# Strassen's seven block products for both matmuls of a gated MLP

## The chip, the core and the metric

The kernel runs on one core of a Trainium2 chip. The core has five engines with queues of their own: TensorE (matmuls from SBUF into PSUM), VectorE, ScalarE, GpSimd (elementwise work; GpSimd has no path to PSUM) and SyncE, whose queue issues all DMA transfers here. The metric is device time in microseconds, the median of three runs.

## What is computed

One decoder layer over 1024 tokens with 1024 channels in float32. A mixing sub-layer (projection, state-space model and short convolution, output projection, norm, residual) comes first and is not changed. Then comes the channel sub-layer, which the change is about:

```python
def conv_ffn(h, w_up, ffn_conv_w, w_down):
    hid = causal_dwconv(h @ w_up, ffn_conv_w)      # 1024 -> 2 x 2816, depthwise, width 3 over tokens
    a, v = jnp.split(hid, 2, axis=-1)
    return (jax.nn.silu(a) * v) @ w_down           # 2816 -> 1024

h = rms_norm(x, g_pre_ffn[i]) * (1.0 + sc2) + sh2
x = x + gt2 * rms_norm(conv_ffn(h, w_up[i], ffn_conv_w[i], w_down[i]), g_post_ffn[i])
```

## The kernel before

Float32 accuracy comes from splitting each operand into a high and a low float32r part and running three matmuls (high x high, high x low, low x high): `mm3`, L460 to 468. The split is a cast on ScalarE (high part) and a subtraction on VectorE or GpSimd (low part). So every operand tile costs one ScalarE and one VectorE or GpSimd step, and every 128x128 by 512 product three matmuls.

The order of the instructions on each engine is written out by a planner, `Flow` (L189 to 295). Every piece of work is a generator, a thread, which yields the engine and an assumed cost before each step. `Flow` advances a clock per engine, takes the step that can start first (ties by the number in `PRIO`), and emits it. `T_` (L363) is a two-operand step that may go to VectorE or GpSimd: the planner gives it to the one that would be done first by the assumed costs (L348 to 361). Engines are taken as independent of each other there. On the chip each engine then runs its queue in that order and waits by semaphores.

Output projection, norms and the MLP's input go by three blocks of tokens: 512, 256, 256 (`blocks`, L1525). `t_h2` (L1642) makes the normed input of the MLP and its split parts, for eight tiles of 128 channels. `t_ahead` (L1734) takes the first three tiles of the up projection for the blocks that are ready, while later blocks are still being normed.

The MLP: `t_ffn` (L2100) runs the up projection tile by tile (128 hidden channels on partitions, 1024 tokens in two PSUM banks, eight steps along the input channels). 22 gate tiles and 22 value tiles are taken in pairs. `t_gate2` (L1826) reads a tile from PSUM: one ScalarE step and four VectorE steps for the convolution (`taps`), a sigmoid, gate times sigmoid on GpSimd, value times gate on VectorE, then the split of the result. After every two pairs `t_down` (L1868) adds their part of the down projection to an accumulator in SBUF: 768 tokens with channels on partitions, 256 tokens with tokens on partitions (`TC`, L29; `down_t`, L1895). The last group of four (`t_down_last`, L1932) goes by blocks of tokens, each followed by the last norm and the residual. PSUM has three slots `big` of two banks and two slots `sm` of one. `weight_threads` (L425) loads weight tiles through three raw buffers and splits them into three buffers `hl`, with one thread per tile in the order of use. `t_x2t` (L1906) turns the residual of the last 256 tokens to rows of tokens, by transposes on TensorE in four groups, through DRAM. `t_ada_last` (L1486) computes the last gate's modulation during the MLP.

Of the kernel before, what the change touches and what calls it, by code (L numbers as in the profile page):

```python
# [25 lines left out]
NT = 4  # L26
GRP = 2
# tokens whose down projection comes out with channels on partitions; the others have tokens there
TC = 768  # L29
NB = (T - TC) // P  # L30
EPS = 1e-6

# columns of the packed per-partition vectors
# [9 lines left out]
# columns of the packed state-space parameters  # L43
# [8 lines left out]
# columns of the packed constants  # L52
# [10 lines left out]
def _constants():  # L63
# [5 lines left out]
    # sin(x) / x and (cos(x) - 1) / x^2 as polynomials in x^2, from the highest power  # L69
# [19 lines left out]
# where the elementwise steps with a choice of engine go  # L89
# [34 lines left out]
    "ada_5": ("dve", "pool"),  # L124
}
# which thread goes first when several could
# [36 lines left out]
    "weights": 13.0,  # L163
}
# [24 lines left out]
class Flow:  # L189
    """Emits the steps of several threads in the order in which their engines could run them.  # L190

    A thread is a generator. It yields ("run", engine, cost) before it emits a step, ("pick", (engine, cost), ...) before
    one that goes to whichever engine is done with it first (and is told which), ("load", queue, cost) before a
    transfer that it doesn't wait for itself, ("wait", event) for another thread, ("get", tag) for a buffer
    slot, ("land",) for its last transfer, and hands slots back with put()."""
# [69 lines left out]
    def _choice(self, th):  # L265
        """start, engine and cost of a thread's next step"""
# [8 lines left out]
    def run(self):  # L275
        while True:
            self._settle()
            ready = [th for th in self.threads if th[4][0] in ("run", "load", "pick")]
# [20 lines left out]
def hybrid_layer(ctx, tc, xT, w_adaT, w_ada0, w_u, w_bcv, w_out, w_up, w_down, glu_w, vec, ssm, con, out):  # L299
    nc = tc.nc  # L300
    outT = out[: D * TC].rearrange("(d t) -> d t", d=D)
    outB = out[D * TC :].rearrange("(b p d) -> b p d", p=P, d=D)
# [9 lines left out]
    psm = ctx.enter_context(tc.tile_pool(name="psm", bufs=2, space=bass.MemoryType.PSUM))  # L312
    mix = ExitStack()
    fp = mix.enter_context(tc.tile_pool(name="k4", bufs=NK4, side="right"))
# [3 lines left out]
    fl = Flow({"k2": NK2, "k4": NK4, "hl": NHL, "raw": NRAW, "big": 3, "sm": 2, "nrm": 2, **{t: 1 for t in tables}})  # L318
# [28 lines left out]
    # estimated engine time of a step over n elements per partition  # L347
# [15 lines left out]
    def T_(site, o, a, b, op, n):  # L363
        """a tensor_tensor where SITES says: on DVE, on GpSimd, or on whichever is done with it first"""
# [6 lines left out]
    def rsqrt(dst, src, inv_n, tmp, eps, n, eps_col=None):  # L371
        """dst = 1 / sqrt(src * inv_n + eps): Newton steps from ScalarE's table, or from the bits' halved exponent"""
# [19 lines left out]
    # ---- constants and small parameters  # L392
# [23 lines left out]
    x2t_dr = tc.dram_tile([NB, P, D], F32, name="x2t_dr")  # L416

    # ---- weight tiles: loaded in the order of their use, split in float32r parts
# [6 lines left out]
    def weight_threads():  # L425
        """one thread per weight tile, in the order of use, so that loads run ahead"""
        prev = None
        for key, src in wq:
            def one_tile(key=key, src=src, prev=prev):
# [30 lines left out]
    def mm3(outs, wh, wl, xh, xl, start, stop):  # L460
        """outs[i] += w^T x[i] in the three passes that carry float32"""
# [11 lines left out]
    def token_rstd(squares, blocks, use, table=True):  # L473
        """1 / rms of each of `blocks` blocks of 128 tokens, on every partition, four at a time in PSUM"""
# [28 lines left out]
    # ---- start. With X = x * g (1 + scale) and the norm's r per token, h = X r + shift, and so the projection  # L503
# [1109 lines left out]
    def t_resid(bi, og4, so):  # L1613
# [17 lines left out]
        for t in s2[1]:  # L1631
            fl.put(t)
# [553 lines left out]
```

## Time and profile before

| | |
|---|---|
| timed runs | 1208.76, 1209.24, 1214.38 us; median 1209.24 |
| profiled execution | 1207.7 us from the first to the last instruction; the page gives no other time of its own |
| mean granted TensorE clock | 0.971 |
| TensorE busy | 1127.5 us, 5654 matmuls |
| VectorE, ScalarE, GpSimd busy | 732.8, 383.2, 402.9 us |
| DMA | 117 MB, mean 97 GB/s |

Busy shares are means over stages: the mixing half ends at about 449 us, the rest is the MLP. In the lists below a row of a timeline gives start, length, engine, line, operation, output and input tiles, shapes, and a count where several are merged. A row of a window gives its bounds and length, then each engine's busy time with instruction counts.

### The profile page before, as it was taken

Reading aid. Unit: us, or ns where it says so; the run is one execution under the profiler, and the core shown is the slowest. Engines: PE = TensorE matmul, PEld = TensorE weight load, DVE = VectorE, ACT = ScalarE, POOL = GpSimd, SP = SyncE. Lnnn points to the kernel's source line nnn. Section 1 sums busy time; section 2 is a strip of 40 time slices with the busy share of each in tenths; the row PEclk is TensorE's granted clock in tenths of the full one; section 3 lists DMA queues with packets and bytes.
Section 4 is the critical chain, followed back from the end, with each engine's and each line's share of the span. In section 5 each row is a group of like instructions: output and inputs, shape, how many; then the busy total and the mean of one; then the engine's idle time right before and its main releaser. Section 6 shows DMA issues by size and latency. Waiting matters only on the chain. (4 is left out here: it accounts for less than half of the span.)

```text
span 1207.7 us, 14269 instructions
## 1 busy us (share of the span) xinstructions
PE 1127.5 (93%) x5654; PEld 931.8 (77%) x5654; DVE 732.8 (61%) x1001; ACT 383.2 (32%) x501; POOL 402.9 (33%) x383
## 2 busy tenths in 40 slices
PE   2887999997999899999999999999999999999994
PEld 2665777775658888888888888888888888888883
DVE  6769877888963897775525434443535254444468
ACT  4445322331544463522212121312122122212252
POOL 4799376625560340412121103021121211120214
PEclk9978989999899989999999999999999999999997
DMA  7634222266442552325221111101121111112203
GB/s 270 231 117 156 80 77 54 86 210 211 157 147 76 177 177 97 122 70 178 84 71 57 40 53 53 53 21 67 36 70 35 53 53 49 39 53 70 88 10 130
DMA packets 54482, 117.02 MB, mean 97 GB/s; under 512 B 5776, under 2 KB 27280, under 8 KB 54416
## 3 DMA queue, kind: packets, MB, share of 16 engines
q1 hardware_dynamic: 54416, 116.12, 28.9%
q8 instruction: 44, 0.72, 0.2%
q14 instruction: 22, 0.18, 0.0%
HBM read 101.97 MB, written 14.13 MB: 96 GB/s over the span
## 5 line engine op out<-in xcount | busy, mean ns | idle before, releaser
L859 DVE SCALAR_TENSOR_TENSOR cv<-big,vec,cv 128x896 f32<-128x896 f32 (+3 forms) x176 | 123.1, 743 | 226.9 <-ACT cv L1821 226.9
L464 PE MATMUL big<-h2h,hl 128*128 128x512 f32 (+1 forms) x728 | 226.4, 384 | 0.0
L468 PE MATMUL big<-h2h,hl 128*128 128x512 f32 (+1 forms) x728 | 225.6, 383 | 0.0
L466 PE MATMUL big<-h2l,hl 128*128 128x512 f32 (+1 forms) x728 | 225.5, 383 | 0.0
L366 POOL TENSOR_TENSOR hl<-w,hl 128x1024 fp32r<-128x1024 f32 x25 | 63.4, 2538 | 313.1 <-ACT hl L450 309.2
L466 PEld LDWEIGHTS big<-h2l,hl 128*128 128x128 f32 x728 | 137.3, 189 | 26.7
L468 PEld LDWEIGHTS big<-h2h,hl 128*128 128x128 f32 x728 | 137.1, 188 | 26.9
L464 PEld LDWEIGHTS big<-h2h,hl 128*128 128x128 f32 x728 | 137.0, 189 | 26.4
L366 DVE TENSOR_TENSOR hl<-w,hl 128x1024 fp32r<-128x1024 f32 x58 | 78.2, 1349 | 58.1 <-ACT hl L450 58.1
L450 ACT CAST hl<-w 128x1024 fp32r<-128x1024 f32 x83 | 86.6, 1043 | 82.3 <-PE big L468 67.1
L1806 POOL TENSOR_TENSOR wd<-w,wd 128x1024 fp32r<-128x1024 f32 x21 | 51.1, 2449 | 168.0 <-ACT wd L1804 168.0
L1821 ACT ACTIVATE cv<-big,vec 128x1024 f32<-128x1024 f32 x44 | 49.0, 1114 | 178.2 <-PE big L468 175.3
L1835 POOL TENSOR_TENSOR cv<-cv,sg 128x1024 f32<-128x1024 f32 x22 | 53.7, 2439 | 123.5 <-ACT sg L1832 123.5
L856 DVE TENSOR_TENSOR acc<-acc,big 128x768 f32<-128x768 f32 (+2 forms) x80 | 69.4, 871 | 40.9 <-PE big L468 40.7
L464 PE MATMUL big<-gh,wd 128*128 128x512 f32 (+1 forms) x336 | 90.1, 338 | 1.2 <-DVE acc L2025 1.2
L466 PE MATMUL big<-gl,wd 128*128 128x512 f32 (+1 forms) x336 | 90.5, 339 | 0.0
L468 PE MATMUL big<-gh,wd 128*128 128x512 f32 (+1 forms) x336 | 90.1, 338 | 0.0
L468 PE MATMUL big<-h,hl 128*128 128x512 f32 x192 | 60.9, 399 | 4.1 <-POOL hl L366 4.1
L1844 ACT CAST gh<-cv 128x512 fp32r<-128x512 f32 x44 | 25.3, 618 | 123.7 <-DVE cv L856 123.7
L464 PE MATMUL big<-yh,hl 128*128 128x256 f32 (+1 forms) x192 | 64.5, 336 | 0.0
L466 PE MATMUL big<-h,hl 128*128 128x512 f32 x192 | 61.2, 399 | 2.3 <-DVE h L714 2.3
L464 PE MATMUL big<-h,hl 128*128 128x512 f32 x192 | 62.4, 407 | 0.9 <-DVE u L856 0.4
(293 smaller groups left out, 1990.1 us busy)
## 6 DMA issues: line engine op xcount, KB each, us to landing
w<-in_w_up_dram SPq DMA_DIRECT2D x44, 512.0 KB, 3.5
w<-in_w_down_dram SPq DMA_DIRECT2D x22, 512.0 KB, 3.5
w<-in_w_out_dram SPq DMA_DIRECT2D x20, 512.0 KB, 3.5
WBT<-in_w_adaT_dram SPq DMA_DIRECT2D x13, 512.0 KB, 4.5
w<-in_w_bcv_dram SPq DMA_DIRECT2D x13, 512.0 KB, 3.9
WB<-in_w_adaT_dram SPq DMA_DIRECT2D x9, 512.0 KB, 4.5
x<-in_xT_dram SPq DMA_DIRECT2D x8, 512.0 KB, 7.0
w<-in_w_adaT_dram SPq DMA_DIRECT2D x8, 512.0 KB, 3.5
```

What stands on the lines that cost most here:

```text
L366: {"dve": dve, "pool": pool}[e].tensor_tensor(o, a, b, op)
L450: act.copy(t[:, 0, :], w)
L464: pe.matmul(outs[i], wh, xh[i], start=start, stop=False)
L466: pe.matmul(outs[i], wh, xl[i], start=False, stop=False)
L468: pe.matmul(outs[i], wl, xh[i], start=False, stop=stop)
L856: (eng or dve).tensor_tensor(o, a, b, op)
L859: dve.scalar_tensor_tensor(o, a, s, b, op0, op1)
L1806: pool.tensor_tensor(hl[:, 1, :], w, hl[:, 0, :].bitcast(F32), SUB)
L1821: act.activation(r, o, AF.Copy, scale=V("ffn_conv_w", 3 * i + 2))
L1835: pool.tensor_tensor(a, a, sg, MUL)
L1844: act.copy(g[0][hf], v[:, sl])
```

## The change

Both matmuls are cut in halves along all three dimensions and computed by the seven products of Strassen's scheme in the form with few additions. For C = A B with blocks A11 to A22 and B11 to B22: S1 = A21 + A22, S2 = S1 - A11, S3 = A11 - A21, S4 = A12 - S2; T1 = B12 - B11, T2 = B22 - T1, T3 = B22 - B12, T4 = B21 - T2; the products are P1 = A11 B11, P2 = A12 B21, P3 = S4 B22, P4 = A22 T4, P5 = S1 T1, P6 = S2 T2, P7 = S3 T3; C11 = P1 + P2, U2 = P1 + P6, T5 = P5 + U2, C22 = T5 + P7, C21 = U2 + P7 + P4, C12 = T5 + P3 (in the up projection the names of the code for the results differ, since its output is transposed).

Up projection: the halves are of the tokens, of the input channels, and gate against value columns. The forms of the input (A11, A12, A22, S1 to S4) are made once, before the MLP, by `t_forms` and `t_forms2`, in steps of 256 tokens for the two later blocks. The weight forms are made per pair of tiles in `t_pair_weights`. `t_up` runs the seven products of a pair, four steps along the channels each, into four PSUM banks; `t_combine` forms the sums with PSUM operands and writes most of them back to PSUM. The convolution and gate follow as before, but the gated tile is not split: it is stored to DRAM.

Down projection: it starts after the whole up projection. Each product runs over 11 steps along the hidden channels for four blocks of 128 tokens and 512 output channels, with its whole sum in PSUM: two sets of four banks in turn. `g_threads` loads the blocks of the gated tiles again for each product, forms their sums, splits them (two steps along k to a chunk; S1 and S2 are stored to DRAM and loaded again); `w_threads` does the same for the weights, which `t_wd` has loaded into SBUF as room comes free. `t_evict` combines the results, `t_half` and `t_final` do the last norm and residual. All output now has tokens on partitions, so `t_x2t` turns the residual of all tokens (16 groups of four transposes). The pools of the mixing half are closed in three stages (`stage`) as the work that needs them is planned: "a" after the last norm's sums, the PSUM slot "v" (in place of the two `sm`) once the last norm scale has been used, "b" after the forms.

```diff
-    AHEAD = (0, NFF, 1)
+    NAHEAD = 3
+    def product(o, w, form, last, s=None):
+        for k in range(NT):
...
+            yield M_(0.6465 if s is None else 0.345)
+            mm3([o], w[0][:, ks], w[1][:, ks], [f[0]], [f[1]], k == 0, k == NT - 1)
...
+    def first_products(i, hl):
+        yield ("get", "big")
+        a = pair_big[i] = big()
+        yield from product(a[:, H:], (hl[:, 0, :H], hl[:, 1, :H]), "A11", i == NFF - 1)
+        fl.fire(ev_p[i, 1])
+        yield from product(a[:, :H], (hl[:, 0, H:], hl[:, 1, H:]), "A12", i == NFF - 1)
+        fl.fire(ev_p[i, 2])
...
+    def t_ahead():
+        yield ("wait", ev_out)
+        for i in range(NAHEAD):
...
+            yield from first_products(i, w[1])
...
+    def t_forms(s, k):
...
+        for o, op, a, b in ((a22, ADD, a21, a22), (a21, SUB, a11, a21), (a11, SUB, a22, a11)):
+            yield from T_("form", o, a, b, op, 256)
+        yield from form_parts("S2", k, s, a11, mod[:, 3, NT + k : NT + k + 1])
...
+    def split(t, w, n):
+        yield A_(n)
+        act.copy(t[:, 0, :n], w)
+        yield from T_("wsplit", t[:, 1, :n], w, t[:, 0, :n].bitcast(F32), SUB, n)
...
+    def t_pair_weights(i):
...
+        yield from T_("wsum", b11, b12, b11, SUB, H)
+        yield from T_("wsum", b12, b22, b12, SUB, H)
...
+        yield from split(ev["b"].tile, wb, 1024)
...
+        yield from T_("wsum", b22, b22, b11, SUB, H)
...
+        yield from split(ev["T2"].tile, b22, H)
...
+        yield from T_("wsum", b21, b21, b22, SUB, H)
...
+        yield from split(ev["t"].tile, wa, 1024)
...
+    def t_up(i):
...
+            yield from product(Z[:, sl], part("T2"), "S2", last, s)
...
+            if not s:
+                yield ("get", ("v", "big")[i % 2])
+                pair_v[i] = big4(i % 2)
...
+            yield from product(W[:, sl], part("t", 0), "S1", last, s)
...
+            yield from product(X[:, sl], part("b", 0), "S3", last, s)
...
+            yield from product(Z[:, sl], part("t", 1), "A22", last, s)
...
+            yield from product(W[:, sl], part("b", 1), "S4", last, s)
...
+    def t_combine(i):
...
+        act.copy(u, Z)
...
+        tt(Y, Y, u, ADD)
...
+            tt(u[:, sl], Z[:, sl], u[:, sl], ADD)
...
+            tt(t5[:, sl], W[:, sl], u[:, sl], ADD)
...
+            tt(u[:, sl], X[:, sl], u[:, sl], ADD)
...
+            tt(X[:, sl], X[:, sl], t5[:, sl], ADD)
...
+            tt(Z[:, sl], Z[:, sl], u[:, sl], ADD)
...
+            tt(W[:, sl], W[:, sl], t5[:, sl], ADD)
...
+            load(g_dr[i], b)
...
+    SUMS = {"S1": ("A21", ADD, "A22"), "S3": ("A11", SUB, "A21"), "S2": ("S1", SUB, "A11"), "S4": ("A12", SUB, "S2")}
...
+    def g_threads():
...
+                    if len(xs) == 2:
+                        yield from T_("gsum", x, x, xs[1], SUMS[form][1], w)
...
+                    yield from split(t, x, w)
...
+    def t_down():
...
+                pe.matmul(o, gh, w[:, 0, :], start=kk == 0, stop=False)
+                pe.matmul(o, gh, w[:, 1, :], start=False, stop=False)
+                pe.matmul(o, gl, w[:, 0, :], start=False, stop=kk == NKK - 1)
...
+    def t_evict(tb):
...
+        yield from T_("gsum", t5, t5, u, ADD, H)
+        yield from T_("gsum", u, u, c22, ADD, H)
+        yield from T_("gsum", c22, c22, t5, ADD, H)
...
+    stage(ev_sp, mix, "a", {"s4": 2 * NT, "sn": NSN, "wf0": 1, "hm0": 1}, side="right")
+    stage(ev_h2s, mixp, "v", {"v": 1}, space=bass.MemoryType.PSUM)
+    stage(ev_forms, mix4, "b", {"cv": NCV, "gs": NGS, "wf1": 1, "hm1": 1}, side="left")
```

In the new `SITES`, the forms, weight sums, splits and down-projection sums (`form`, `wsum`, `wsplit`, `gsum`, `dsum`) may go to VectorE or GpSimd; the gate is listed for GpSimd alone, as before.

More of the change, by code (lines that the diff above doesn't have):

```diff
@@ L26 @@
 NT = 4
-GRP = 2
-TC = 768
-NB = (T - TC) // P
+NKK = NFF // 2
+NB = T // P
 EPS = 1e-6
@@ L124 @@
     "ada_5": ("dve", "pool"),
+    "form": ("dve", "pool"),
+    "wsplit": ("dve", "pool"),
+    "wsum": ("dve", "pool"),
+    "gate": ("pool",),
+    "gsum": ("dve", "pool"),
+    "gsplit": ("dve", "pool"),
+    "dsum": ("dve", "pool"),
 }
@@ L1770, in hybrid_layer @@
     fl.spawn(t_xr(), PRIO["t_xr"])
-    fl.run()
-    mix.close()
-    NCV, NWD, NG = 5, GRP + 1, 4
-    ffp = ctx.enter_context(tc.tile_pool(name="ffn", bufs=1, side="right", reuse_waits="tile"))
-    acc = [ffp.tile([P, TC], F32, name=f"acc{d}") for d in range(KD)]
-    acc_t = [ffp.tile([P, D], F32, name=f"acct{b}") for b in range(NB)]
-    now = max(fl.free.values())
-    fl.slots.update(cv=[now] * NCV, wd=[now] * NWD, g=[now] * NG)
-    fl.cur = [0, 0, None, fl.free["pe"], None, 0.0, None]
@@ new lines, in hybrid_layer, with gs_tile, s4_tile, t_half @@
+    fin = cp.tile([P, NB, 4], F32, name="fin")
+    half = {}
+    ev_half = {(b, c): Event() for b in range(NB) for c in range(2)}
+    ev_colb = Event()
+    def gs_tile():
+        return ptile("b", "gs", [H], F32, NGS)
+    def s4_tile(s):
+        return ptile("a", "s4", [H], F32, 2 * NT)
+    def t_half(b, c, u, tag):
+        yield ("get", "gs")
+        q = gs_tile()
+        yield A_(H + 100)
+        act.activation(q, u, AF.Square, accum_out=fin[:, b, c : c + 1])
+        fl.put("gs")
+        yield ("wait", ev_colb)
+        yield D_(H)
+        tt(u, u, cbc[:, c * H : (c + 1) * H], MUL)
+        half[b, c] = u, tag
+        fl.fire(ev_half[b, c])
@@ new lines, in t_final @@
+    def t_final(b):
+        for ev in [ev_half[b, 0], ev_half[b, 1]] if b < NTB else [ev_G["P3", NKK - 1], ev_prod["P3", NTB - 1]]:
+            yield ("wait", ev)
+        yield ("wait", ev_x2t)
+        yield ("get", "cv")
+        x = cv("x")
+        yield L_(512)
+        load(x, x2t_dr[b])
+        yield ("land",)
+        for c in range(2):
+            yield ("wait", ev_half[b, c])
+        f = fin[:, b, :]
+        yield D_(1)
+        tt(f[:, 0:1], f[:, 0:1], f[:, 1:2], ADD)
+        r = f[:, 1:2]
+        yield from rsqrt(r, f[:, 0:1], 1.0 / D, (f[:, 2:3], f[:, 3:4]), EPS, 1, C("eps", 0, 1))
+        for c in range(2):
+            sl = slice(c * H, (c + 1) * H)
+            u, tag = half[b, c]
+            yield D_(H + 60)
+            stt(x[:, sl], u, r, x[:, sl], MUL, ADD)
+            fl.put(tag)
+            yield L_(256)
+            load(outB[b, :, sl], x[:, sl])
+        yield from t_put()
@@ new lines, in t_put, with t_ada_last @@
+    def t_put():
+        yield ("land",)
+        fl.put("cv")
+    def t_ada_last():
+        yield ("wait", pw[NFF - 1]["t"])
+        for k in range(KD):
+            yield ("get", "raw")
+            w = wp.tile([P, D], F32, tag="raw", name=nm("w"))
+            yield L_(512)
+            load(w, w_adaT[5 * D + k * P : 5 * D + (k + 1) * P, :])
+            yield from t_ada_dot(5, k, w, "raw")
+        yield L_(100)
+        load(col_dr.rearrange("(k p) -> p k", p=P), col[:, 3, :])
+        yield ("land",)
+        yield L_(512)
+        load(cbc, col_dr.unsqueeze(0).to_broadcast([P, D]))
+        yield ("land",)
+        fl.fire(ev_colb)
@@ new lines, in t_all_up @@
+    def t_all_up():
+        for i in range(NFF):
+            yield from t_up(i)
+        yield from t_down()
+    fl.spawn(t_tsh(), PRIO["t_resid"])
+    for s in range(2):
+        for k in range(NT):
+            fl.spawn(t_forms(s, k), PRIO["forms"][s])
+    for i in range(NFF):
+        fl.spawn(t_pair_weights(i), PRIO["weights"])
+    fl.spawn(t_x2t(), PRIO["t_x2t"])
+    fl.spawn(t_all_up(), PRIO["t_ffn"])
+    fl.spawn(t_gate2(), PRIO["t_gate2"])
+    for i in range(NFF):
+        fl.spawn(t_combine(i), PRIO["t_combine"])
@@ new lines, in hybrid_layer, with stage @@
+    g_threads()
+    fl.spawn(t_wd(), PRIO["t_wd"])
+    w_threads()
+    fl.spawn(t_ada_last(), PRIO["t_ada_dot"])
+    for tb in range(NTB):
+        fl.spawn(t_evict(tb), PRIO["t_evict"])
+    for b in range(NB):
+        fl.spawn(t_final(b), PRIO["t_final"])
+    def stage(until, close, key, slots, **kw):
+        fl.run(until=until)
+        close.close()
+        pools[key] = ctx.enter_context(tc.tile_pool(name=f"ff{key}", bufs=1, reuse_waits="tile", **kw))
+        for tag, n in slots.items():
+            fl.slots[tag] += [until.t] * n
```

762 lines of the change are left out of this document (434 added, 328 removed).

## The prediction

> **What bounds the kernel now.** I read the page first, then the busy time by stage, then the spacing of single matmuls. Page, and the stages of the gated MLP (window, its length, busy time of PE, PEld, DVE, ACT and POOL with instruction counts, granted clock, DMA share, GB/s):
>
> ```profile
> span 1207.7 us, 14269 instructions
> PE 1127.5 (93%) x5654; PEld 931.8 (77%) x5654; DVE 732.8 (61%) x1001; ACT 383.2 (32%) x501; POOL 402.9 (33%) x383
> ...
> 449.30:470.60 21.30, 19.35 (x84) 15.68 (x83) 18.85 (x36) 10.83 (x22) 4.80 (x2) 0.92 0.18 55
> 470.60:489.00 18.40, 18.40 (x155) 18.36 (x155) 11.39 (x25) 8.33 (x14) 2.41 (x1) 1.00 0.27 95
> 489.00:1166.30 677.30, 676.13 (x3191) 566.08 (x3190) 318.11 (x394) 168.53 (x193) 125.94 (x52) 1.00 0.20 63
> 1166.30:1196.00 29.70, 24.48 (x147) 21.54 (x145) 25.25 (x46) 11.39 (x26) 15.89 (x12) 0.89 0.22 81
> 1196.00:1207.70 11.70, 0.00 (x0) 0.00 (x0) 8.30 (x20) 2.04 (x7) 4.76 (x5) 0.64 0.44 157
> ```
>
> The MLP's first product starts at 449.3 and 758.4 us of the span follow. From 489 to 1166 TensorE never rests at full clock, VectorE is busy 47% and GpSimd 19%: the stage is bound by matmuls. What one costs is read from their starts (start, length, engine, line, what); a row's length overlaps the next:
>
> ```profile
> 450.68 0.39 PE L464 MATMUL big<-h2h,hl 128*128 128x512 f32 x1
> ...
> 457.26 0.39 PE L468 MATMUL big<-h2h,hl 128*128 128x512 f32 x1
> ...
> 470.65 0.28 PE L464 MATMUL big<-h2h,hl 128*128 128x256 f32 x1
> ...
> 471.72 0.95 PE L480 MATMUL sm<-con,CL 128*128 128x1 f32 x8
> ...
> 699.77 0.62 PE L464 MATMUL big<-h2h,hl 128*128 128x512 f32 x2
> ...
> 707.93 0.39 PE L464 MATMUL big<-h2h,hl 128*128 128x512 f32 x1
> ```
>
> Between the last two rows lie 36 matmuls of 512 columns, 0.2267 us each. Between the first two, with new weights for every output, 29, also 0.227: the other loop order of the change costs nothing. Nine of 256 columns take 1.07, 0.12 each.
>
> **The matmuls removed.** Up projection before: 2040 of 512 columns and 144 of 256, 462.5 + 17.3 = 479.8 us. Down projection: 780 and 552 (768 tokens make a 512 and a 256 for each output), 176.8 + 66.2 = 243.0. Together 722.8 of the 758.4. The rest: 6.1 in 449 to 489 (39.7 less 33.6 of products), 7.2 until 1166, 22.2 after that, of which 11.7 follow the last matmul. After: up 22 pairs x 7 products x 12 = 1848, of which pair 0 runs 60 in halves: 1788 x 0.2267 + 120 x 0.12 = 419.7. Down 7 x 11 x 12 = 924: 209.5. Sum 629.2, so 93.6 us less. The question is what the other engines let through. The work ahead of 449.3 stays.
>
> **The shared read path of VectorE and GpSimd.** Every block sum and every split of the change is a two-operand step on these two. Their rows:
>
> ```profile
> 428.43 0.68 DVE L366 TENSOR_TENSOR og<-og,CL 128x512 f32<-128x512 f32 x1
> 429.03 0.68 DVE L366 TENSOR_TENSOR og<-og,Tr 128x512 f32<-128x512 f32 x1
> ...
> 430.83 2.70 DVE L859 SCALAR_TENSOR_TENSOR h2l<-og,mod,h2h 128x512 fp32r<-128x512 f32 x1
> 433.45 2.92 DVE L366 TENSOR_TENSOR CL<-CL,Tr 128x512 f32<-128x512 f32 x1
> ...
> 437.50 0.74 DVE L859 SCALAR_TENSOR_TENSOR h2l<-og,mod,h2h 128x512 fp32r<-128x512 f32 x1
> ...
> 440.75 0.73 DVE L859 SCALAR_TENSOR_TENSOR og<-og,col,sm 128x512 f32<-128x512 f32 x1
> ```
>
> ```profile
> 430.57 2.41 POOL L366 TENSOR_TENSOR hl<-w,hl 128x1024 fp32r<-128x1024 f32 x1 [2.96 <-DVE og L366]
> 433.43 2.39 POOL L366 TENSOR_TENSOR hl<-w,hl 128x1024 fp32r<-128x1024 f32 x1 [0.45 <-ACT hl L450]
> 440.67 2.41 POOL L366 TENSOR_TENSOR hl<-w,hl 128x1024 fp32r<-128x1024 f32 x1 [4.84 <-ACT hl L450]
> ```
>
> VectorE steps with both operands in SBUF (430.83, 433.45) take 2.70 and 2.92 instead of 0.74 and 0.68, and end just after GpSimd's. The one with an operand in PSUM (440.75, tile sm) runs beside GpSimd at 0.73. So two-SBUF steps of VectorE and GpSimd's steps shut each other out. Where both have a backlog they alternate:
>
> ```profile
> 107.95 4.79 DVE L714 SCALAR_TENSOR_TENSOR h<-x,mod,h 128x512 fp32r<-128x512 f32 x3
> ```
>
> ```profile
> 107.44 3.05 POOL L366 TENSOR_TENSOR cy<-La,ssm 128x512 f32<-128x512 f32 x2
> ```
>
> One of each takes 1.56 us, no faster than both on VectorE (0.66 + 0.60). A step given to GpSimd thus holds the path 0.9 / 0.60 = 1.5 to 2.4 / 1.13 = 2.1 times as long, while the kernel's planner counts the engines as independent. Prices from starts: 512 elements 0.60 (rows 428.43, 429.03), 1024 elements 1.13, four conv steps of a tile 2.64:
>
> ```profile
> 484.65 2.72 DVE L859 SCALAR_TENSOR_TENSOR cv<-big,vec,cv 128x896 f32<-128x896 f32 x4 [3.51 <-ACT cv L1821]
> 487.29 1.83 DVE L366 TENSOR_TENSOR hl<-w,hl 128x1024 fp32r<-128x1024 f32 x1
> ...
> 1022.63 1.21 DVE L366 TENSOR_TENSOR hl<-w,hl 128x1024 fp32r<-128x1024 f32 x1
> 1023.76 1.66 DVE L859 SCALAR_TENSOR_TENSOR cv<-big,vec,cv 128x127 f32<-128x127 f32 x3
> ```
>
> The Trainium skill states it as a rule (SBUF — State Buffer, Who interferes with whom): a VectorE instruction with two SBUF inputs and a GpSimd instruction that reads SBUF cannot run together, and the later one blocks fully. The rows above agree. By the rule without overlap the two terms below would be +52 and +55, which is the slow rival; without the rule they would be near zero.
>
> **Up stage, per pair of tiles.** TensorE 84 x 0.2267 = 19.04 us. VectorE must: 7 combine steps from PSUM (4.2), the conv steps of two tiles (5.3), value times gate (1.13): 10.6. With a choice of engine: 4 weight sums (2.4), splits of 3 x 1024 and one 512 (4.0): 6.4. All on VectorE 17.0; the gate keeps GpSimd busy for 2.4 in any case. If GpSimd also gets 30% of the choices (1.9, 3.9 us of its time), VectorE has 15.1 left plus what it is blocked, at most GpSimd's 6.3: 15.1 to 21.4, halfway 18.2. Below 19.04, but nearly full. Cover for a late step: t5 and u2 have two products, 5.4 us; weights are about a pair ahead, limited by the three split buffers. Bounds for 22 pairs: 0 and 22 x 2.36 = 52. The nearest row has VectorE at 94% and GpSimd at 40%, and TensorE lost 3%:
>
> ```profile
> 240.00:260.00 20.00, 19.42 (x121) 15.48 (x118) 18.75 (x30) 5.45 (x6) 8.05 (x12) 1.00 0.47 154
> ```
>
> 3% of 419.7 is 12. I take +12. Added ScalarE casts and the store of each gated tile lie beside TensorE.
>
> **Down stage, per product.** TensorE 132 x 0.2267 = 29.9. On VectorE alone the splits of G and W take 5.5 x 1.13 + 11 x 0.60 = 12.8; P5 and P7 add one sum of each operand (6.2 + 6.6 = 25.6), P6 6.2 + 13.2 (32.2, already over 29.9), P3 6.2 plus P6's evictions (28.6 and 2.4 from PSUM). Only one or two chunks fit ahead (three G and two W buffers), so a short product cannot pay for a long one. With a quarter on GpSimd at 1.75 the path takes 1.19 times: losses P5 5.8 (with P2's evictions), P7 0.5, P6 8.4, P3 6.5: 21. Bounds: all on VectorE 4; 40% at 2.1 55. I take +21, since a quarter is what an almost full VectorE leaves over. P1, P2 and P4 are covered; so is the start, as PSUM of pair 20 is free a pair earlier.
>
> **Into the MLP.** Before, the three tiles taken ahead have 33.6 us of products for 1.5 blocks while the later blocks are normed. Now they have 72 products, 16.3 us. Pair 0 then needs pool "a" (after the last norm), and its fifth product a PSUM slot that opens only when the last norm scale is used (second view):
>
> ```profile
> 459.59 1.05 PE L480 MATMUL sm<-con,oq 128*128 128x1 f32 x8 [1.95 <-DVE oq L366]
> ...
> 462.82 0.63 PE L466 MATMUL big<-h2l,hl 128*128 128x512 f32 x1
> ...
> 464.53 0.63 PE L468 MATMUL big<-h2h,hl 128*128 128x512 f32 x1
> ```
>
> ```profile
> 479.19 0.87 DVE L859 SCALAR_TENSOR_TENSOR og<-og,col,sm 128x256 f32<-128x256 f32 x2
> ```
>
> So from about 470 to 480 there are 1.4 us of products: 8 to 9 us idle; the forms add 22.6 us of VectorE work (eight times 2.8, at 0.34 to 0.39 for 256 elements, half of the rows' 0.60 and a fixed part), delaying that by some 3; restarting at half clock (matmuls 0.43 apart between 462.82 and 464.53) costs 1.7. +13, bounds 4 and 30. The usual 6 for norms between products stays.
>
> **The residual turned to rows of tokens** goes from 4 to 16 groups of transposes, which stand in TensorE's queue with all products behind them. Each waits for a load that waits for the store before it:
>
> ```profile
> 545.51 0.60 PE L1923 MATMUL sm<-con,x 128*128 128x128 f32 x4
> ```
>
> ```profile
> x<-x_dr SPq DMA_DIRECT2D x4, 256.0 KB, 3.5
> x2t_dr<-xt SPq DMA_DIRECT2D x4, 256.0 KB, 2.8
> ```
>
> The planner allows 2.83 for each (line 181 and the size); the load lands 0.7 later. 16 x 0.45 of work and half of 16 x 0.9 of waiting: +14. Bounds: 7, and 30 if weight loads ahead of it on SP's queue wait for buffers.
>
> **Tail.** Four token blocks end 2.0 us apart, each with 3.4 us of VectorE work, then the store. The last block before took 4.2 from its PSUM read to its last product, then 3.1 to the end:
>
> ```profile
> 1200.47 0.41 DVE L856 TENSOR_TENSOR acct<-acct,big 128x256 f32<-128x256 f32 x1
> ...
> 1203.11 1.54 DVE L859 SCALAR_TENSOR_TENSOR u<-u,nrm,xt 128x512 f32<-128x512 f32 x3
> ```
>
> 4 x 3.4 - 6 + 3.1 is about 11 after the last matmul (bounds 9 and 14). The 10.5 of gaps ahead of it go.
>
> **Sum** against the profiled span: 449.3 + 629.2 + 6 + 13 + 14 + 12 + 21 + 11 = 1155.5, 52 below 1207.7. The median of the runs is 1.5 above that span: 1157.
>
> **Rivals.**
> Dense: VectorE's PSUM steps hide GpSimd's, every term falls to its low bound (4, 7, 0, 4, 9): 1108.5 and 1.5, 1110. For it: VectorE alone fits every stage but P6. Against: both engines were never this full without gaps.
> Shut out (the other side): the planner gives GpSimd 30% of the up stage's choices and 40% of the down stage's, each of its steps holds VectorE for its whole length, and 21.4 us a pair set the pace: +40 and +34 over the forecast, 1231. It decides from 20.4 us a pair with the down stage at its bound. For it: rows 430.83 and 433.45. Against: 9.5 of VectorE's 17 us read PSUM.
> Transfers: during P5 0.79 MB must move per 2.7 us of products, 290 GB/s, near the most seen,
>
> ```profile
> 0.00:20.00 20.00, 5.49 (x24) 5.05 (x24) 10.84 (x22) 6.74 (x9) 9.14 (x8) 1.00 0.90 330
> ```
>
> and P6 the same. If that and the transposes' loads (16 more) cost 10 each in P5 and P6, 1193.
>
> **How the numbers follow.** Forecast 0.52 (its own range 1130 to 1182), dense 0.20, transfers 0.16, shut out 0.12. Faster by over 0.5% (below 1203): the first three, 0.88; within 0.5%, about what a measurement here can tell from no change: 0.03 of the last; slower 0.09. The range 1118 to 1206 leaves out the far ends.
>
> **What would show it.** Right: 2712 MLP matmuls of 512 columns, 0.227 apart; TensorE near full in the up stage at about 19.5 us a pair; gaps in P5, P6 and P3 released by VectorE or GpSimd splits; two-SBUF steps of 2 us and more beside GpSimd. Wrong: gaps released by DMA, a halved clock inside a stage, or up pairs over 20.4 us.

## The result and the profile after

The changed kernel takes 1282.18 us (median of 4 runs, 1277.57 to 1285.25) against 1209.0 for the kernel before beside it. The ratio is 1.0593, 95% interval 1.0555 to 1.0631: slower by 6%, where 1157 was forecast. Its profiled execution (total, and busy time of the engines):

```profile
span 1283.5 us, 13975 instructions
...
PE 1091.5 (85%) x5000; PEld 856.3 (67%) x5000; DVE 998.5 (78%) x1327; ACT 478.5 (37%) x662; POOL 474.1 (37%) x440
```

TensorE has 654 matmuls fewer and 36 us less busy time, and is busy 85% of the span instead of 93%. The products were saved; the time came back as gaps. The stages of the MLP, by window (length; busy time of PE, PEld, DVE, ACT, POOL; granted clock; DMA share; GB/s): up to the first product, pairs 0 to 2, pairs 3 to 21, down projection, tail.

```profile
449.30:460.08 10.78, 7.00 (x37) 6.53 (x37) 10.78 (x22) 7.47 (x14) 5.90 (x4) 0.68 0.73 230
460.08:567.38 107.30, 78.18 (x354) 63.23 (x352) 87.10 (x137) 42.86 (x75) 44.49 (x33) 0.81 0.26 85
567.38:1000.82 433.44, 387.21 (x1628) 298.45 (x1629) 345.30 (x430) 148.30 (x166) 94.48 (x48) 1.00 0.27 94
1000.82:1268.00 267.18, 231.88 (x925) 181.40 (x923) 200.06 (x226) 99.16 (x165) 85.18 (x46) 0.93 0.58 193
1268.00:1283.50 15.50, 0.17 (x1) 0.00 (x0) 10.94 (x33) 1.50 (x5) 0.00 (x0) 0.62 0.67 237
```

The first product starts 10.8 us later than before. Against matmuls at 0.2267 us (0.12 for 256 columns), pairs 0 to 2 lose 107.3 - 57.9 = 49.4, pairs 3 to 21 lose 433.4 - 19 x 19.04 = 71.7, the down stage 267.2 - 209.5 = 57.7, and 15.5 follow the last matmul. With the 449.3 of the start and the 629.2 of products that is 1283.6, the whole span: these are the places to explain.

**The steady up stage.** From pair 6 on a pair takes 22.4 to 22.6 us, at full clock. Matmuls of one such pair where a gap opens (start, length, engine, line, what; in brackets idle time and its releaser):

```profile
745.75 0.50 PE L480 MATMUL v<-s,hl 128*128 128x512 f32 x1 [0.78 <-DVE sn L872]
...
757.79 0.50 PE L480 MATMUL big<-h2h,hl 128*128 128x512 f32 x1 [0.68 <-ACT sn L2005]
...
759.97 0.39 PE L480 MATMUL big<-s,wf 128*128 128x512 f32 x1
760.19 0.39 PE L482 MATMUL big<-s,wf 128*128 128x512 f32 x1
760.42 0.39 PE L484 MATMUL big<-s,wf 128*128 128x512 f32 x1
761.67 0.50 PE L480 MATMUL big<-s,wf 128*128 128x512 f32 x1 [0.86 <-DVE big L872]
```

There are three gaps, in P7, P2 and P6, each after the first k step (three matmuls) of its product. The starts 760.42 and 761.67 are 1.25 apart where 0.23 is usual. What VectorE does there:

```profile
760.91 0.70 DVE L872 TENSOR_TENSOR big<-big,sn 128x512 f32<-128x512 f32 x1 [1.80 <-PE big L484]
```

This is Y + u. It reads and writes the half Y of the pair's PSUM tile while P6 adds to the half Z. It had been idle and waited for P6's first k step; P6's second k step waits for it. No number passes between the two. In the program each such matmul carries a wait on VectorE's or ScalarE's semaphore. In P7 the step is t5 = W + u, which reads W while P7 writes X; in P2 it is ScalarE's copy of Z while P2 writes Y. The two halves are two banks of 512 floats; the Trainium skill (PSUM — Partial Sum Buffer, Terms) names a collision only for two engines on the same bank, so by it nothing in the chip asks for this wait. No run here shows what the chip would do without it.

The groups of the stage that carry waits (pairs 3 to 21; columns: operation, count, busy time, mean, idle before it and releasers):

```profile
L480 PE MATMUL big<-h2h,hl 128*128 128x512 f32 x152 | 61.9, 407 | 15.5 <-ACT sn L2005 13.3 <-ACT xt L2103 2.2
...
L480 PE MATMUL big<-s,hl 128*128 128x512 f32 x80 | 32.7, 409 | 7.8 <-DVE sn L872 7.8
L480 PE MATMUL big<-s,wf 128*128 128x512 f32 x76 | 31.9, 420 | 15.9 <-DVE big L872 15.9
```

With the even pairs' P7 (tile v, 7.1) the three kinds (15.9, 13.3 and 7.8) make 44 us of recorded idle time. Each gap costs about 1.05 from start to start, three of them 3.15 a pair; the rest of the 3.45 that a pair loses is spacing, 0.230 instead of 0.2267.

**The down stage.** Per product, P1 P2 P5 P7 P6 P3 P4: 31.8, 39.1, 44.6, 33.3, 40.5, 41.5, 36.4 us, each with 29.9 of matmuls.

### The profile page after: what moved, and what is told of

It reads as the page before. It is cut to its first block, busy times and chain, and to the rows that moved or that the text cites. A ratio compares the mean times of both kernels' runs of the same rounds, so it can differ in the third digit from the quotient of the medians.

```text
span 1283.5 us, 13975 instructions
## 1 busy us (share of the span) xinstructions
PE 1091.5 (85%) x5000; PEld 856.3 (67%) x5000; DVE 998.5 (78%) x1327; ACT 478.5 (37%) x662; POOL 474.1 (37%) x440
## 4 chain that ended last, share of the span: by engine, by line
PE 38%; DVE 8%; DMA 3%; issue 2%; ACT 2%; POOL 1%; DVEq 0%; SPq 0%; POOLq 0%; ACTq 0%
PE big L480 8%; PE big L484 7%; PE big L482 7%; PE big L2265 2%; PE big L2266 2%; PE big L2264 2%; PE v L480 2%; PE v L484 2%; PE v L482 2%; DMA w<-in_w_adaT_dram 1%; DVE sn L872 1%; PE v L2265 1%; PE v L2266 1%; DVE big L872 1%; PE v L2264 1%
## 5 line engine op out<-in xcount | busy, mean ns | idle before, releaser
L1895 ACT CAST hl<-w 128x1024 fp32r<-128x1024 f32 (+1 forms) x83 | 84.0, 1013 | 266.4 <-PE big L2266 106.7
L384 DVE TENSOR_TENSOR hl<-w,hl 128x1024 fp32r<-128x1024 f32 (+1 forms) x100 | 127.5, 1275 | 53.6 <-ACT hl L1895 33.6
L384 POOL TENSOR_TENSOR hl<-w,hl 128x1024 fp32r<-128x1024 f32 (+1 forms) x25 | 65.0, 2604 | 135.4 <-ACT hl L466 96.6
L384 POOL TENSOR_TENSOR cv<-cv,cv 128x1024 f32<-128x1024 f32 x22 | 59.2, 2691 | 118.4 <-ACT cv L2067 118.4
L2265 PE MATMUL big<-hm,hl 128*128 128x512 f32 x220 | 90.5, 411 | 10.6 <-DVE hm L384 8.3
L2264 PE MATMUL big<-hm,hl 128*128 128x512 f32 x220 | 90.5, 412 | 5.6 <-ACT hm L1895 4.8
L2266 PE MATMUL big<-hm,hl 128*128 128x512 f32 x220 | 89.3, 406 | 0.0
L480 PE MATMUL big<-h2h,hl 128*128 128x512 f32 x176 | 73.2, 416 | 16.0 <-ACT sn L2005 13.3
L872 DVE TENSOR_TENSOR big<-big,sn 128x512 f32<-128x512 f32 (+1 forms) x67 | 46.0, 689 | 50.2 <-PE big L484 50.2
L482 PE MATMUL big<-h2l,hl 128*128 128x512 f32 x176 | 70.2, 399 | 0.0
L484 PE MATMUL big<-h2h,hl 128*128 128x512 f32 x176 | 70.1, 398 | 0.0
L480 PE MATMUL big<-yh,hl 128*128 128x256 f32 (+1 forms) x192 | 65.1, 339 | 1.1 <-ACT hl L466 1.1
L484 PE MATMUL big<-yh,hl 128*128 128x256 f32 (+1 forms) x192 | 63.1, 329 | 2.0 <-POOL hl L384 2.0
L482 PE MATMUL big<-yl,hl 128*128 128x256 f32 (+1 forms) x192 | 62.9, 327 | 0.0
```

The source lines that it names most:

```text
L384: {"dve": dve, "pool": pool}[e].tensor_tensor(o, a, b, op)
L480: pe.matmul(outs[i], wh, xh[i], start=start, stop=False)
L482: pe.matmul(outs[i], wh, xl[i], start=False, stop=False)
L484: pe.matmul(outs[i], wl, xh[i], start=False, stop=stop)
L872: (eng or dve).tensor_tensor(o, a, b, op)
L1895: act.copy(t[:, 0, :n], w)
```

## The experiments

Where no interval is given a time is one execution; the kernel before took 1210.2 to 1210.6 beside these runs. The four executions of the changed kernel lie 7.7 us apart, so a single total that differs by less says little; the lengths of the stages come from the traces.

**The order of the products.** P5 (into W) is put ahead of P6 (into Z), and every reader of a tile comes when TensorE writes another one: ScalarE's copy of Z and Y + u during P5, Z + u during P7, the sums on W and X during P4:

```
-            yield from product(Z[:, sl], part("T2"), "S2", last, s)
             yield from product(W[:, sl], part("t", 0), "S1", last, s)
+            yield ("wait", snap[i, "c11", s])
+            yield from product(Z[:, sl], part("T2"), "S2", last, s)
...
-            yield ("wait", snap[i, "t5", s])
+            yield ("wait", snap[i, "c22", s])
             yield from product(W[:, sl], part("b", 1), "S4", last, s)
...
-        yield ("wait", ev_p[i, 1])
+        yield ("wait", ev_p[i, 2])
         Y, Z = pair_big[i][:, :H], pair_big[i][:, H:]
...
-            yield ("wait", ev_p[i, 5, s])
+            yield ("wait", ev_p[i, 7, s])
             W, X = pair_v[i][:, :H], pair_v[i][:, H:]
```

> The same seven products per pair of the up projection with the same sums and splits, but in the order P1 P2 P5 P6 P7 P4 P3, and ScalarE's copy and VectorE's sums placed so that none of them reads a two-bank PSUM tile while TensorE writes into it. Nothing is left out. Theory A (same tile): the three stalls of about 1.05 us in each steady pair come from a dependency on the whole two-bank tile. Then pairs 3 to 21 go from 22.8 us to 19.1 to 19.7 each, and the total from 1282 to about 1222. Theory B (shared read path): the sums and splits of VectorE and GpSimd, which are the same as before, set the pace; the pairs stay at 22 to 23 us and the total within 5 us of 1282.

1239.24 us. The pairs from 8 on take 20.0 us and pairs 3 to 21 391.2, 42 less; the start, the first pairs and the down stage differ by less than 4. Theory A holds, but short of its numbers (19.1 to 19.7 a pair, 1222 in all): a pair is still 1.0 over its matmuls. One wait is left, in front of P3, for the sums on X; in VectorE's queue these stand behind a long step (first fence TensorE, second VectorE):

```profile
788.70 0.50 PE L480 MATMUL big<-s,hl 128*128 128x512 f32 x1 [0.64 <-DVE big L872]
```

```profile
785.99 1.45 DVE L872 TENSOR_TENSOR cv<-cv,cv 128x1024 f32<-128x1024 f32 x1
787.36 0.68 DVE L872 TENSOR_TENSOR sn<-big,sn 128x512 f32<-128x512 f32 x1
787.97 1.28 DVE L872 TENSOR_TENSOR big<-big,sn 128x512 f32<-128x512 f32 x2
```

The last row holds two steps, and the first of them is X + t5. It touches X, and P3 writes W of the same tile.

**All choices on VectorE.** This takes GpSimd out of the sums and splits:

```
-    "form": ("dve", "pool"),
-    "wsplit": ("dve", "pool"),
-    "wsum": ("dve", "pool"),
+    "form": ("dve",),
+    "wsplit": ("dve",),
+    "wsum": ("dve",),
...
-    "gsum": ("dve", "pool"),
+    "gsum": ("dve",),
...
-    "dsum": ("dve", "pool"),
+    "dsum": ("dve",),
```

> All block sums and operand splits with a choice of engine on VectorE, none on GpSimd (the gate stays there). Nothing is left out. Theory A (same tile): the steady pairs keep their three stalls and stay at 22 to 23 us; what changes is only where VectorE is full, in the first three pairs (107 us) and in the down stage's P5, P6 and P3. Theory B (shared read path): GpSimd's share of these steps costs VectorE more than it saves; the steady pairs fall to 20 to 21 us, the first three pairs by 10 us or more, the down stage from 267 to about 250, the total to about 1215. If instead the two engines add up as independent ones, the down stage grows, to about 280, and the total to about 1295.

1315.75 us, 34 slower. From pair 8 on a pair takes 23.5 to 25.0 us, the down stage 284.8; pairs 0 to 2 take 5 less (102.0). Theory B falls as an account of the pace: with only the gate left on GpSimd, the stage is slower. The pairs also leave the 22 to 23 us of theory A, and the down stage is nearer to the 280 that were put down for two engines that add up as independent ones. Busy time in 700 to 860 us, the changed kernel first, then this one:

```profile
700.00:860.00 160.00, 142.99 (x596) 110.24 (x597) 133.06 (x164) 52.96 (x57) 28.82 (x14) 1.00 0.21 73
```

```profile
700.00:860.00 160.00, 139.86 (x567) 104.16 (x565) 122.61 (x162) 49.31 (x56) 16.58 (x7) 0.99 0.20 68
```

At 22.5 us a pair the first is 18.7 us of VectorE and 4.1 of GpSimd; at 23.75 the second is 18.2 and 2.5. So the steps given to GpSimd hardly relieve VectorE's busy time, as the prediction's price had it, and that did not set the pace either way. The slower pace shows at least in part in TensorE's waits: the three gaps are still there (16.5 us in these 160, 16.9 before), and it now also waits 3.7 us for the low part of T2's split on VectorE, once in each of seven pairs. That fits splits that come later when VectorE makes them all.

**The residual's transposes later.** One wait is added to their thread:

```
     def t_x2t():
+        yield ("wait", pw[4]["T2"])
```

> The residual's 16 groups of transposes with their loads and stores start only when the weights of pair 4 are split, not during the output projection. Nothing is left out. Theory C (the transposes stand in TensorE's queue at the start of the MLP): the first MLP product starts at 450 to 453 us, not 460, the first three pairs take 95 to 100 us, not 107, the total falls by 15 to 20, to about 1264. Theory D (VectorE is full with the forms and the norm there, the transposes only fill its gaps): the first product stays near 458 and the total within 5 us of 1282.

1287.91 us. The first product starts at 452.14 instead of 460.08, as theory C had it, but pairs 0 to 2 take 109.5 and pairs 3 to 21 442.1, 8.7 more. TensorE waits 5.2 us there for PSUM that the transposes' copies hold, where it waited 2.2. Later transposes cost no less, only in another place.

**Eight products in the down projection.** With the up stage as changed, the down stage takes each half of the tokens through 22 k tiles, one G tile of 128 x 512 and one w_down tile of 128 x 1024 at a time, into all eight banks:

```
+        for r in range(2):
...
+            for k, tb in order:
...
+                for i, (x, y) in enumerate(((gh, 0), (gh, 1), (gl, 0))):
+                    for c in range(2):
+                        cs = slice(c * H, (c + 1) * H)
+                        pe.matmul(banks[tb][:, cs], x, w[:, y, cs], start=k == 0 and i == 0, stop=k == NFF - 1 and i == 2)
```

> Up projection as in the changed kernel; the down projection in eight block products: 22 k tiles for each half of the tokens, the whole sum of 4 token blocks of 1024 columns in PSUM, each k tile of G split once, each of w_down once per half. 1056 matmuls of 512 columns (239.4 us at 0.2267) instead of 924 (209.5). Nothing is left out. Theory E (operand work sets the down stage): without the forming of sums the products run at their spacing, 240 to 246 us instead of 267, the total about 1258. Theory F (transfers at the stage's start, or the PSUM of the last pairs, set it): the first 60 us still lose 10 us or more, the stage takes 255 to 265 and the total stays above 1270.

1275.27 us, the stage 264.4 us, with 239.4 of matmuls. Of the 25 lost, 15 lie before 1040, in the first 115 of 1056 matmuls. That is theory F as it was put; without the sums, the products still do not run at their spacing. The largest gap there, and VectorE's queue ahead of it:

```profile
1015.88 6.38 PE L2198 MATMUL big<-hm,hl 128*128 128x512 f32 x18 [8.59 <-DVE cv L875]
```

```profile
1006.43 2.73 DVE L636 SCALAR_TENSOR_TENSOR w<-w,cbc 128x1024 f32<-128x1024 f32 x1 [1.97 <-DMA w<-in_w_adaT_dram]
1009.09 0.08 DVE L636 DVE_READ_ACCUMULATOR w<-w,cbc 128x1 f32 x1
1009.09 1.14 DVE L875 SCALAR_TENSOR_TENSOR cv<-big,vec,cv 128x896 f32<-128x896 f32 x1
1012.92 1.23 DVE L636 SCALAR_TENSOR_TENSOR w<-w,cbc 128x1024 f32<-128x1024 f32 x1 [2.69 <-DMA w<-in_w_adaT_dram]
```

The rows of w_ada for the last gate stand in VectorE's queue between the last pair's convolution steps, and each waits for its load; the PSUM of that pair comes free late. The changed kernel has the same rows in P1, and a wait for a load of G in P2 (first fence VectorE, second TensorE):

```profile
1030.36 1.23 DVE L636 SCALAR_TENSOR_TENSOR w<-w,cbc 128x1024 f32<-128x1024 f32 x1 [2.63 <-DMA w<-in_w_adaT_dram]
...
1056.62 1.23 DVE L384 TENSOR_TENSOR w<-w,cv 128x1024 f32<-128x1024 f32 x1 [7.71 <-DMA cv<-g_dr]
```

```profile
1058.50 0.80 PE L2265 MATMUL big<-hm,hl 128*128 128x512 f32 x1 [4.41 <-DVE hm L384]
```

A sum for P5 waits 7.7 us for its load of G, and the split that P2 needs stands behind it in VectorE's queue.

**Later sums, earlier w_ada rows.** On top of the new order:

```
-            yield ("wait", snap[i, "c22", s])
+            yield ("wait", snap[i, "t5", s])
             yield from product(W[:, sl], part("b", 1), "S4", last, s)
...
             fl.fire(snap[i, "t5", s])
+            yield ("wait", ev_p[i, 3, s])
             yield D_(n)
             tt(u[:, sl], X[:, sl], u[:, sl], ADD)
...
-        yield ("wait", pw[NFF - 1]["t"])
         for k in range(KD):
+            yield ("wait", pw[5 + 2 * k]["T2"])
```

> As the run with the new order of the up products (the order run, 1239), with two more edits. P3 waits for one sum (t5 = W + u) instead of three: the two sums that read X and the one that reads Z are made after P3. And the eight rows of w_ada for the last gate are loaded and reduced one per two pairs in the up stage, not at its end. Nothing is left out. Theory A (same tile): the 0.6 to 1.0 us that a steady pair still loses in front of P3's last products goes, pairs 3 to 21 take 365 to 372 us, not 391. Theory G (the w_ada rows stand in VectorE's queue, each waiting for its load, ahead of the last pairs' convolution and the first splits of the down stage): P1 and P2 together fall from 72 to 60 to 63 us; total about 1207. Rival H (the transfers of w_down and G at the stage's start are slow by themselves): P1 and P2 stay at 70 or more, total about 1217.

1223.9 us. The steady pairs take 19.1 to 19.8 (19.3 in the mean of pairs 7 to 19, 19.04 of matmuls), and from 700 to 860 TensorE is busy without a break:

```profile
700.00:860.00 160.00, 159.86 (x696) 130.28 (x695) 150.95 (x185) 61.81 (x68) 54.57 (x26) 1.00 0.26 92
```

VectorE is at 94% here, busier than the 83% of the changed kernel, with GpSimd at 34%. So neither engine's load was the cause of the stalls: with the same steps, placed so that no reader meets a writer of its tile, they are gone. Tiles of one bank each, which would show it with the order left alone, were not tried. Pairs 3 to 21 still take 387.2, where 365 to 372 were expected: pairs 3 to 5 lose 15.5 us, 6.4 of it waiting for a PSUM slot that the transposes' copies hold (releaser ACT xt), the last two pairs 5.2. P1 and P2 take 63.8 instead of 70.9, near theory G's 60 to 63. The edit takes both the VectorE steps and 4 MB of loads out of the stage, and no run tells the two apart. P2, in the changed kernel and here, speaks more for the loads (the last two columns are DMA share and GB/s):

```profile
1032.65:1071.79 39.14, 33.72 (x132) 26.49 (x133) 18.34 (x23) 12.47 (x19) 4.46 (x3) 0.91 0.94 282
```

```profile
977.40:1009.30 31.90, 31.06 (x132) 24.79 (x133) 16.89 (x19) 12.32 (x19) 5.80 (x4) 1.00 0.61 199
```

Over P1 and P2 VectorE waits 11.1 us for loads of G in the changed kernel, and 2.9 here; for the rows of w_ada themselves it waited 4.0 there.

The same with the eight products of the down projection above:

> As the run before it in this list, with the down projection in eight block products of 239.4 us in all. Nothing is left out. Theory G: with the w_ada rows out of the way the last pairs' PSUM comes free in time, the down stage takes 240 to 248 us (264 in the run with eight products and late w_ada rows); total 1180 to 1190, a ratio of 0.975 to 0.985 to the kernel before the change. Rival H: the stage keeps some 20 us of gaps in its first 50 us; total about 1205.

1218.75 us, ratio 1.0058 (1.0031 to 1.0085). The stage takes 257.9, 10 more than the most expected, and the total misses theory G's 1180 to 1190 by 29. The wait for the last pair's convolution falls from 12.2 to 6.3 us, so theory G was half of that wait; 4.8 us go to splits of w_down, which have two tiles of lead.

**No sums in the down stage.** The edit drops the lines that form S and T in P5, P7, P6 and P3 (those of P6's weights are not shown), so the output is not the layer's:

```
-                        yield from T_("gsum", x, x, xs[1], SUMS[form][1], w)
...
-                                yield from T_("dsum", w, wd[other, kk], w, SUB, H)
```

> As the first of this list, but the block sums of the down stage are left out (P5, P7 and P6 take the first of their loaded blocks unsummed, P3 too; the loads, the stores of the formed blocks and all splits stay), so its output is not the layer's. Theory I (the forming of sums on VectorE and GpSimd sets P5, P7, P6 and P3, as the prediction had it): these four go from about 161 us to 122 to 126, the loss of 41 us falls to a few. Rival J (the short lead of the operands, two chunks of w_down and three of G, makes every late step a gap, whatever the sums cost): they stay above 140.

1205.77 us. P5 falls from 44.2 to 34.0, P6 from 41.8 to 31.0, P7 from 33.2 to 32.5; P3 stays, 41.9 and 43.0. Down products P5, P7, P6, P3 with the sums (the run before with early w_ada rows), then without:

```profile
1009.30:1053.50 44.20, 33.84 (x134) 26.25 (x132) 35.47 (x36) 15.80 (x29) 15.17 (x9) 0.88 0.49 169
1053.50:1086.70 33.20, 31.21 (x132) 24.59 (x132) 27.48 (x28) 13.90 (x22) 11.20 (x7) 1.00 0.66 220
1086.70:1128.50 41.80, 36.03 (x133) 27.63 (x133) 34.35 (x34) 12.56 (x18) 20.18 (x11) 0.88 0.48 169
1128.50:1170.40 41.90, 34.39 (x134) 26.42 (x132) 32.20 (x32) 14.66 (x26) 17.69 (x10) 0.92 0.34 112
```

```profile
1013.30:1047.30 34.00, 30.99 (x133) 24.45 (x131) 17.72 (x22) 15.26 (x29) 3.63 (x3) 1.00 0.61 205
1047.30:1079.80 32.50, 31.02 (x133) 24.74 (x133) 14.08 (x17) 13.72 (x22) 1.84 (x1) 1.00 0.67 227
1079.80:1110.80 31.00, 30.77 (x132) 24.87 (x133) 13.88 (x17) 11.90 (x18) 3.22 (x2) 1.00 0.65 226
1110.80:1153.80 43.00, 35.39 (x134) 27.68 (x133) 28.97 (x31) 14.63 (x26) 14.62 (x8) 0.88 0.33 112
```

The four take 140.5 together, just past the 140 set for rival J and far from theory I's 122 to 126. So theory I holds for P5 and P6, 21 us together, and not for the rest. In P3 another thing counts, and it is still there without the sums. The trace points to the eviction of P6; no run took it away. From 1109.7 to 1131 VectorE does nothing but the 20 steps of it, among them (second fence GpSimd)

```profile
1113.97 3.45 DVE L384 TENSOR_TENSOR sn<-sn,z 128x512 f32<-128x512 f32 x2
1117.35 1.28 DVE L384 TENSOR_TENSOR z<-z,s 128x512 f32<-128x512 f32 x2
...
1122.05 5.66 DVE L384 TENSOR_TENSOR sn<-sn,z 128x512 f32<-128x512 f32 x2
```

```profile
1111.78 5.09 POOL L384 TENSOR_TENSOR hm<-wd,hm 128x512 fp32r<-128x512 f32 x3
...
1121.55 5.62 POOL L384 TENSOR_TENSOR hl<-w,hl 128x1024 fp32r<-128x1024 f32 x2
```

where two steps that cost 1.28 alone take 3.45 and 5.66 beside GpSimd's splits, and the splits for P3 come after them.

**No transposes.** On top of the run with eight products and early w_ada rows (1218.75) the residual is added unturned, so the output is not the layer's:

```
-    fl.spawn(t_x2t(), PRIO["t_x2t"])
-        load(x, x2t_dr[b])
+        load(x, x2_dr[b * P : (b + 1) * P, :])
```

> As the second of this list, but the residual is not turned to rows of tokens: its 16 groups of transposes, their copies, loads and stores are left out, and the last step adds blocks of the untransposed residual, so the output is not the layer's. Theory C (the transposes cost what the prediction said, about 14 us, in the output projection and the first pairs): first MLP product at 450 to 452, pairs 0 to 2 in 95 to 100 us, total 12 to 18 below that run. Theory D (VectorE's backlog of norm, forms and splits sets the start, the transposes fill gaps): the first product moves by up to 5 us, pairs 0 to 2 stay at 103 to 107, the total falls by less than 6.

1205.45 us, 13.3 less. The amount is theory C's; the place is not: the first product comes 3.8 us earlier, pairs 0 to 2 take 2 more, and pairs 3 to 21 7 less, the down stage 5 less. In the first three pairs the transposes did fill gaps, as theory D had it.

**Two pairs ahead, not three,** on the same run:

```
-    NAHEAD = 3
+    NAHEAD = 2
```

> As the run with eight products in the down projection (1218.75, pairs 0 to 2 in 106.1 us), with one number changed: the first two products of two pairs, not three, are made ahead of the forms. Nothing is left out. Theory M (PSUM is full: with three pairs begun, pair 1's second two-bank tile must wait until pair 0's convolution has read its own, the gap of 12 us between 519 and 531): 5.4 us of products fewer ahead, that gap gone, pairs 0 to 2 in 96 to 100 us, total 1208 to 1213. Theory K (VectorE's backlog of norm, forms and splits sets the time until 530): pairs 0 to 2 stay at 104 us or more, total 1216 or more.

1201.98 us, 16.8 less. Pairs 0 to 2 take 96.6 instead of 106.1; the two windows show the gap that closes (with three ahead, then with two):

```profile
520.00:540.00 20.00, 9.93 (x33) 7.65 (x33) 15.34 (x20) 8.49 (x9) 3.64 (x2) 0.66 0.29 95
```

```profile
520.00:540.00 20.00, 19.28 (x89) 15.71 (x88) 17.46 (x24) 8.67 (x11) 6.08 (x3) 1.00 0.36 105
```

Theory M. As much again comes in pairs 3 to 21 (377.6 for 387.1), all of it in pairs 3 to 5, where the wait for the transposes' copies falls from 6.1 to 0.7 us.

**No forms,** again on that run; S1 to S4 and their low parts are not made, so the output is not the layer's:

```
-            yield from T_("form", o, a, b, op, 256)
...
-            yield from T_("form", lo, u, hi.bitcast(F32), SUB, 256)
...
+            f[1] = f[0]
```

> As the run with eight products in the down projection (1218.75), but the sums that form S1 to S4 and their low parts are left out: ScalarE's copies stay, TensorE takes the high part for both, so the output is not the layer's. VectorE and GpSimd lose some 40 us of work between 440 and 510. Theory K: the gaps from 487 to 503 (6.2, 4.8 and 1.6 us) close and pairs 0 to 2 take 88 to 95 us, total 1203 to 1208. Theory M: the last norm scale and pair 0's convolution set them; pairs 0 to 2 take 100 us or more, total 1212 or more.

1198.28 us. Pairs 0 to 2 take 90.4, 15.7 less: theory K as well. Of the three gaps that were to close, the first stays (5.9 us, released by the last norm scale on VectorE), the second goes and the third grows from 1.6 to 2.5. The 12 us gap that two pairs ahead close is still open here, so these are two separate causes.

**All that helped.** The order, the late sums, the early w_ada rows, two pairs ahead, and eight products in the down projection with a longer lead of the operands:

```
+    KA = 4
...
+                    if n > 4:
+                        yield ("wait", used[n - 5])
...
+                    yield ("get", "k2", 4)
+                    t = [[r2("w"), r2("w")] for _ in range(2)]
```

> All that helped together, nothing left out: the up products in the new order with the late sums, the w_ada rows early, two pairs ahead, the down projection in eight products with up to five k tiles of w_down and six of G split ahead in single-bank-wide buffers, and four k tiles of the first two token blocks ahead of the other two, so that the last pairs' PSUM may come late. Theories G, M and A together: down stage 241 to 246 us (257.9 without the longer lead), pairs 0 to 2 at 96 to 100, total 1188 to 1198, a ratio of 0.98 to 0.99 to the kernel before the change. If the down stage's gaps have another cause (clock, transfers), it stays above 252 and the total above 1203.

1190.23 us, ratio 0.9827 (0.9807 to 0.9847) to the kernel before: 1.7% faster. The up projection by Strassen pays, with the down projection in eight products. The down stage and the tail:

```profile
937.00:1180.20 243.20, 241.58 (x1056) 199.02 (x1056) 107.71 (x190) 82.06 (x161) 5.00 (x3) 0.99 0.44 157
1180.20:1189.40 9.20, 0.19 (x1) 0.00 (x0) 5.35 (x15) 1.67 (x5) 0.00 (x0) 0.63 0.37 143
```

TensorE is busy 241.6 of 243.2 us.

**Both in seven products, mended.** The edits of the run with later sums and early w_ada rows, and NAHEAD = 2:

> The change as given, both projections in seven block products, with the three mends of the up stage together: the new order of the products with the late sums, the w_ada rows early, two pairs ahead. The down stage's operands are formed, split and led as in the changed kernel. Nothing is left out. If the mends add up (1223.9 for the first two, 16.8 less for two pairs ahead), the total is 1204 to 1210, a ratio of 0.995 to 1.001: seven products in both projections are worth no more than the kernel before, and the down stage, 261 us against 209.5 of products, is what is left of the loss. If pairs ahead gained only because of the eight products' down stage, the total stays above 1215.

1211.58 us (10 runs), ratio 0.9999 (0.9983 to 1.0016), where 1204 to 1210 was expected. The three mends of the up stage nearly add up, and what they leave is the down stage at 259.8 for 209.5 of products: seven products there are 17 us slower than eight with a longer lead. Seven products with that lead were not run.

## Why the prediction was wrong

The direction was wrong, and the error of 128 us on the sum (1283.5 for 1155.5) lies in every term but the matmuls:

- **Products removed** (629.2): right. 1788 up matmuls of 512 and 120 of 256, 924 down; spacing 0.230 where 0.227 was taken, 0.3 us a pair.
- **Up stage, +12**: 71.7 in pairs 3 to 21. This is the step that failed. The text worked out how full VectorE is ("15.1 to 21.4, halfway 18.2") and read the loss off a stage with VectorE that full. The size was right: VectorE has 18.2 us a pair once the stalls are gone (150.95 us in 8.3 pairs). But then TensorE loses 0.3 us a pair, and with the stalls it lost 3.45 with VectorE less full. What was not asked of the code is which step reads a PSUM tile that TensorE is writing. "Cover for a late step: t5 and u2 have two products" counted the data alone; the tile is one thing for the waits, and three steps, ScalarE's copy and two of the seven sums, fall inside a product that writes its other half. The new order takes 42 of the 71.7 us away, the later sums 4 more; of the 25.4 left, 20.7 are pairs 3 to 5 and the last two, the rest spacing.
- **Into the MLP, +13, the usual 6 and the transposes, +14**: 60 measured (10.8 and 49.4). The transposes' 14 was right in size (13.3 without them), but not in place: most of it came in pairs 3 to 21 and in the down stage, so the agreement is in part luck. The idle time "from about 470 to 480" was there, but later and longer: the forms were said to delay it "by some 3" and cost 15.7 (measured with eight products in the down stage, as the 13.3 was), and nothing was said of PSUM, where three pairs begun leave no tile for pair 1's second half until pair 0 is convolved (9.5).
- **Down stage, +21**: 57.7. Named rightly: P5, P6 and P3, and the reasons, sums in P5 and P6 and, by the trace alone, P6's evictions in P3; they measured 14.7, 10.6 and 11.6 for 5.8, 8.4 and 6.5. Wrong: "P1, P2 and P4 are covered; so is the start". P2 lost 9.2, 7 of it by the w_ada rows and their loads, which the change moves to the start of the down stage and which the prediction did not follow; P4 lost 6.5. Six of the seven products begin by waiting for splits of w_down (1.4 to 2.3 us in their first twelve matmuls), which fits the short lead of the operands; no run changed the lead alone.
- **Tail, +11**: 15.5. VectorE works for 11.4 us after the last matmul, where the sum left 7.6 (4 x 3.4 - 6), and 4.0 lie between its last step and the end, for 3.1. No run looked into it.
- **The rivals.** Shut out, 1231, was on the right side with the wrong mechanism: with the choices taken from GpSimd the kernel got slower. Transfers put its price in P5 and P6; the busiest transfers were in P1 and P2 (0.88 to 0.94 of the engines), with the loads of the w_ada rows among them. The Trainium skill's rule (SBUF — State Buffer, Who interferes with whom) that a VectorE step with two SBUF inputs and a GpSimd step that reads SBUF shut each other out agrees with the steps of 3.45 and 5.66, and with 18.7 against 18.2 us of VectorE a pair; it was only not what set the pace of the up stage.
- **What would show it**: "up pairs over 20.4 us" was named as wrong, and came: 22.5. Of the signs named as right, the 2712 matmuls and the gaps in P5, P6 and P3 behind splits came too.

## What to carry to other kernels

Before summing up engine loads, write down for every accumulator which engine touches which tile while a matmul group writes it: a wait goes with the tile, not with the bytes, and an order in which readers come while another tile is written was worth 2.5 us of 22.5 a pair, and 3.2 with the later sums. A product saved is worth its matmuls only if the operands' sums fit beside the remaining ones; in the down projection leaving out the sums of P5 and P6 gave 21 us back, where the product saved is worth 29.9. Whether a longer lead would make room for them is open. And what moves past a stage's end (here rows that wait for their loads) must be followed through the in-order queue that it now stands in, and through the transfers beside it.

## What was not expected of the hardware

VectorE at 94% and GpSimd at 34% left TensorE no idle time in 160 us; the prediction had read a 3% loss off a stage with VectorE at 94% and GpSimd at 40%. The matmuls of the up stage start 0.230 us apart, those of the kernel before 0.2267; with the stalls gone it is 0.2277 for the first two products, and 0.2267 or 0.233 for the other five, by product and pair, 0.230 in the mean. Why is open.
